# Hybrid decoder layer: the forgetting heads' bias is prepared on GpSimd without the query's factor, and ScalarE multiplies it in

## The chip, the cores and the metric

The kernel runs on one core of a Trainium2 chip. The metric is device time in microseconds (us) of one execution, the median of several. An execution's own time is a little longer than its span in the profile, which runs from the first to the last instruction of the program. The engines are named as the profile names them: PE is TensorE (PEld its weight loads), DVE is VectorE, ACT is ScalarE, POOL is GpSimd, SP is SyncE, which here only issues DMAs.

## The reference

One decoder layer over 512 tokens of width 2048, in float32: RMSNorm, one input projection, two groups of eight attention heads, an output projection with residual, a second RMSNorm and a SwiGLU feed-forward layer of width 5632 with residual. Eight heads (the NSA group) have compressed, selected and windowed branches. The other eight are the forgetting heads ("FoX"), and these are what the change is about:

```python
qf = _rms_norm(qf.reshape(B, T, Hf, Dh), fox_q_norm)
kf = _rms_norm(kf.reshape(B, T, Hf, Dh), fox_k_norm)
log_f = jax.nn.log_sigmoid(ff.astype(f32) + fox_forget_bias.astype(f32))
cum_f = jnp.transpose(jnp.cumsum(log_f, axis=1), (0, 2, 1))
...
s = jnp.einsum("bqhd,bkhd->bhqk", qf_b, kf).astype(f32) * scale
s = s + cq[..., None] - cum_f[:, :, None, :]
p = _masked_softmax(s, key_pos[None, :] <= tpos[:, None])
o_fox = jnp.einsum("bhqk,bkhd->bqhd", p.astype(dt), vf)
```

So each score gets a bias, the difference of two cumulative sums (of the query and of the key), and a causal mask, before the softmax.

## The kernel before

**Stages.** Up to about 370 us the kernel projects its input and runs the eight NSA heads beside it. From there to about 630 us it projects the forgetting heads' queries, keys and values, a pair of projections per head (`ps_kf`, `ps_qf`, `ps_vf`), and weaves the attention of the head before into them. Then comes the output projection (`po`), and from about 780 us the feed-forward layer (`q`, `pd`). Matrices are kept as a high and a low float32r part, so each product is three matmuls, and the large products are made by schemes with fewer multiplications whose operands are sums of blocks.

**One forgetting head.** `fox(h)` (L1005) first loads the row of cumulative sums, broadcast to 128 partitions, into `ckb` (one buffer for all heads; its DMA is issued from ACT's queue). `Branch.scores` (L737) then goes through the four blocks of 128 queries from the last, which has 512 keys, to the first, which has 128 (384 and 256 between). Per block: three matmuls write the scores `s_f` into a PSUM bank (two banks in turn, tag `s`); `nbs(i)` (L1010) makes the bias `nbf`; a DVE instruction reads both, scales by the query's factor, writes `p_f` and a row minimum `st_f`; ACT takes the exponential. So the matmuls of the third block need the bank of the first, and wait until DVE has read it. After the four blocks ACT multiplies `p_f` by the reciprocal sums (four instructions), PE transposes (`pT_f`) and multiplies by the values (`of`).

**The query's factor.** The queries are not normalised before the scores. `factors` (L590) makes, from the column sums `ss_qf`, the factor `qs` by which DVE multiplies at the end and its inverse `iqs`, by which the bias must be multiplied first. `qs_qf` is the tile of both. In `nbs` POOL adds the query's sum to `ckb` and multiplies by `iqs` in one TENSOR_SCALAR, then an AFFINE_SELECT writes a large number above the diagonal in the last 128 columns. There are two `nb` buffers.

**POOL's queue.** POOL also issues DMAs that add up blocks of weights in DRAM (`fsum`, `osum`, L279). Each is made to wait for a weight split on ACT, so that they are spread over the time; what stands behind one in POOL's queue waits with it.

**The order of instructions.** `Ordered` (L178) records what each of the five engines is given up to the end of the attention, and lays it out by five written lists of numbers (`ORDERS`, in the order PE, DVE, ACT, POOL, SP), at the top of the file. An engine works its list in order; the semaphores follow from the data. Behind that the order is the program's.

Of the kernel before, what the change touches and what calls it, by code (L numbers as in the profile page):

```python
# [10 lines left out]
F32 = mybir.dt.float32  # L11
FR = mybir.dt.float32r
AF = mybir.ActivationFunctionType
OP = mybir.AluOpType
# [4 lines left out]
P = 128  # L19
D = 2048  # L20
T = 512
# [3 lines left out]
NB = T // P  # L25
# [7 lines left out]
BIG = 1e30  # L33
# [192 lines left out]
def hybrid_layer(ctx: ExitStack, tc: tile.TileContext, xT, vec, ffb, wfg, wfirst, win, cmpw, wout, wos, wgu, wdn, out):  # L226
# [10 lines left out]
    def act(*args, **kw):  # L237
        return pin(sca.activation(*args, **kw))
# [13 lines left out]
    ap_ = att2.enter_context(tc.tile_pool(name="att", bufs=1))  # L252
# [2038 lines left out]
```

## Time and profile before

| | us |
|---|---|
| median of three executions (lowest to highest) | 2020.66 (2020.0 to 2022.35) |
| the profiled execution's own time | 2018.89 |
| its span | 2017.2 |
| PE busy | 1994.9 (99%) |
| DVE busy | 1794.1 (89%) |
| ACT busy | 1082.4 (54%) |
| POOL busy | 327.6 (16%) |

How to read it: matmuls overlap in the records and their ends are modelled, so PE's idle time in the profile is the time in which nothing at all was in flight. A wait is put down to the instruction whose semaphore came last. In a timeline the first column is the start in us from the span's start, the second the time that the merged group took, "x3" the number of instructions, and the bracket the engine's idle time before the group with what ended it.

### The profile page before, as it was taken

The page shows a single profiled execution, that of the slowest core. Times are in us where ns is not written, and L with a number is a line of the kernel's source. Part 1 is how long each engine was busy: PE and PEld are TensorE (multiplying, and loading weights), DVE is VectorE, ACT ScalarE, POOL GpSimd, SP SyncE. Part 2 cuts the span into 40 slices and gives each one's busy share as a digit, 9 for nine tenths or more (in the row PEclk, how much of TensorE's full clock was granted, in tenths as well). Part 3 has the DMA queues.
Part 4 walks back from the last instruction along what each step waited for, and adds up shares of the span by engine and source line. Part 5 has one row for each costly group of instructions (what it writes and reads, how often), then busy time and mean ns, then how long its engine had stood idle before and what let it go on. Part 6 is the DMA issues. An engine that isn't in the chain of part 4 may idle for free.

```text
span 2017.2 us, 36451 instructions
## 1 busy us (share of the span) xinstructions
PE 1994.9 (99%) x14341; PEld 1885.5 (93%) x14341; DVE 1794.1 (89%) x2725; ACT 1082.4 (54%) x1430; POOL 327.6 (16%) x481
## 2 busy tenths in 40 slices
PE   9999999999999998999999999999999999999999
PEld 8988989899998998999999999999999988888887
DVE  7788889898879777999999999999999998888897
ACT  6566566567676454444444443444444455666564
POOL 1132332423221011111111111111111000001000
PEclk9999999999999999999999999999999999999999
DMA  6676787967785674677767778778777798579974
GB/s 220 229 179 178 188 187 181 233 194 199 223 230 164 229 242 151 172 210 205 220 199 207 224 200 204 224 199 214 210 190 200 218 356 287 160 234 319 354 201 140
DMA packets 154062, 432.39 MB, mean 214 GB/s; under 512 B 18777, under 2 KB 26969, under 8 KB 153890
## 3 DMA queue, kind: packets, MB, share of 16 engines
q1 hardware_dynamic: 102176, 297.60, 44.7%
q0 software_dynamic: 44560, 106.19, 25.3%
q10 hardware_dynamic: 7154, 26.27, 3.4%
q8 instruction: 112, 1.84, 0.4%
q14 instruction: 60, 0.49, 0.1%
HBM read 393.54 MB, written 128.73 MB: 259 GB/s over the span
## 4 chain that ended last, share of the span: by engine, by line
PE 85%; issue 5%; DVE 4%; ACT 2%; POOL 2%; DMA 2%; SPq 0%; ACTq 0%; POOLq 0%; DVEq 0%
PE q L187 38%; PE pd L187 20%; PE po L187 8%; PE ps_qn L187 4%; PE ps_vf L187 2%; PE ps_vs L187 2%; PE ps_first L187 2%; PE on L187 2%; DVE bigm L187 1%; PE ps_kf L187 1%; POOL nbf L187 1%; PE ps_kw L187 1%; PE ps_ks L187 1%; PE s_s L187 1%; PE s_w L187 1%
## 5 line engine op out<-in xcount | busy, mean ns | idle before, releaser
L187 ACT ACTIVATE bigm<-r 128x1792 fp32r<-128x1792 f32 x174 | 299.2, 1720 | 416.7 <-PE q L187 273.5
L187 DVE TENSOR_TENSOR bigm<-r,bigm 128x1792 fp32r<-128x1792 f32 x174 | 351.2, 2019 | 2.6 <-ACT bigm L187 2.1
L187 DVE TENSOR_TENSOR r<-r 128x512 f32<-128x512 f32 x522 | 266.2, 511 | 20.5 <-DMA r<-wgu 8.4
L187 POOL DMA_DIRECT2D wsum<-wdn x176 | 120.3, 690 | 695.7 <-ACT bigm L187 602.2
L187 PE MATMUL q<-forma,bigm 128*128 128x256 f32 x1848 | 215.6, 276 | 4.5 <-ACT bigm L187 2.5
L187 PEld LDWEIGHTS q<-forma,bigm 128*128 128x128 f32 x1848 | 211.3, 193 | 5.3 <-ACT bigm L187 2.9
L187 PE MATMUL q<-formy,bigm 128*128 128x256 f32 x1848 | 214.1, 275 | 1.4 <-ACT bigm L187 1.1
L187 PE MATMUL q<-formx,bigm 128*128 128x256 f32 x1848 | 213.9, 275 | 0.0
L187 PE MATMUL q<-bigm 128*128 128x256 f32 x1848 | 213.8, 275 | 0.0
L187 PEld LDWEIGHTS q<-formy,bigm 128*128 128x128 f32 x1848 | 210.0, 192 | 1.8 <-ACT bigm L187 1.3
L187 PEld LDWEIGHTS q<-formx,bigm 128*128 128x128 f32 x1848 | 210.3, 192 | 0.0
L187 PEld LDWEIGHTS q<-bigm 128*128 128x128 f32 x1848 | 210.0, 192 | 0.2 <-DVE bigm L187 0.2
L187 PE MATMUL pd<-bigm 128*128 128x512 f32 x900 | 202.4, 379 | 0.0
L187 PEld LDWEIGHTS pd<-bigm 128*128 128x128 f32 x900 | 170.1, 189 | 24.2
L187 DVE TENSOR_TENSOR bigm<-wd,bigm 128x1024 fp32r<-128x1024 f32 (+1 forms) x62 | 107.7, 1738 | 21.5 <-ACT bigm L187 21.4
L187 ACT ACTIVATE bigm<-wd 128x1024 fp32r<-128x1024 f32 (+1 forms) x62 | 90.9, 1466 | 31.4 <-DMA wd<-wsum 26.3
L187 ACT ACTIVATE bigm<-rawm 128x768 fp32r<-128x768 f32 (+2 forms) x72 | 65.8, 923 | 64.6 <-PE pd L187 39.3
L187 PE MATMUL pd<-bigm,formx 128*128 128x512 f32 x444 | 99.3, 379 | 0.0
L187 PEld LDWEIGHTS pd<-bigm,formx 128*128 128x128 f32 x444 | 83.9, 189 | 11.9
L187 PE MATMUL po<-bigm,wp_o 128*128 128x512 f32 (+1 forms) x464 | 91.9, 348 | 0.7 <-DVE bigm L187 0.7
L187 DVE TENSOR_TENSOR bigm<-rawm,bigm 128x768 fp32r<-128x768 f32 (+2 forms) x72 | 75.5, 1058 | 16.8 <-ACT bigm L187 16.5
L187 PEld LDWEIGHTS po<-bigm,wp_o 128*128 128x128 f32 x464 | 76.8, 190 | 9.2 <-DVE bigm L187 1.1
(498 smaller groups left out, 3743.8 us busy)
## 6 DMA issues: line engine op xcount, KB each, us to landing
r<-wgu SPq DMA_DIRECT2D x174, 512.0 KB, 4.2
wsum<-wdn POOLq DMA_DIRECT2D x176, 256.0 KB, 5.0
rawm<-ad SPq DMA_DIRECT2D x44, 512.0 KB, 7.1
wd<-wdn SPq DMA_DIRECT2D x40, 512.0 KB, 5.9
wd<-wsum SPq DMA_DIRECT2D x40, 512.0 KB, 6.7
ad<-cb ACTq DMA_DIRECT2D x22, 896.0 KB, 5.9
fsump<-win POOLq DMA_DIRECT2D x72, 256.0 KB, 5.4
rawm<-ad SPq DMA_DIRECT2D x44, 384.0 KB, 3.4
```

The lines of the kernel that those rows point to most:

```text
L187: r = f(*args, **kw)
```

## The change

`fox(h)` now makes the biases of all four blocks when the head begins, in a dictionary `bias`, and without the query's factor: POOL adds (and multiplies by 1.0) and masks. `nbs(i)`, called where the scores are made, multiplies the finished bias in place on ACT by `iqs`, with an ACTIVATE Copy that has a scale per partition. The bias of 256 keys gets a buffer of its own (`nb1`), and that of 128 keys takes the last 128 columns of the buffer of the 384 keys, so that a head's four biases fit at one time. Four of the five lists of the order are written anew (SP's is the same).

```diff
--- before.py
+++ after.py
-0+1 6+4 2+2 91 11+1 99 5 13 15 14 17 20 18 16 19 22 21 23 26 29 24 32 25 28 27 35 38 41 30 44 31 34 33 47 50 37
+0+1 6+3 3+1 91 11+1 99 10 2 5 13 15 14 17 20 18 16 19 22 21 23 26 29 24 32 25 28 27 35 38 41 30 44 31 34 33 47
...
+        bias = {}
+        for i in reversed(range(NB)):
+            n = P * (i + 1)
+            if i == 1:
+                nbt = ap_.tile([P, 2 * P], F32, tag="nb1", name=f"nbf{h}{i}", bufs=1)
+            elif i > 1:
+                nbt = both = ap_.tile([P, T], F32, tag="nb", name=f"nbf{h}{i}", bufs=2)
+            nb = bias[i] = nbt[:, :n] if i else both[:, 3 * P:]
+            pool.tensor_scalar(nb, ck[:, :n], ncq[:, i, h:h + 1], 1.0, op0=OP.add, op1=OP.mult)
+            pool.affine_select(nb[:, n - P:], nb[:, n - P:], pattern=[[-1, P]], compare_op=OP.is_ge,
+                                    fill=BIG, base=0, channel_multiplier=1)
+
         def nbs(i):
-            n = P * (i + 1)
-            nb = ap_.tile([P, T], F32, tag="nb", name=f"nbf{h}{i}", bufs=2)
-            pool.tensor_scalar(nb[:, :n], ck[:, :n], ncq[:, i, h:h + 1], q[2][:, i:i + 1] if len(q) == 3 else 1.0, op0=OP.add, op1=OP.mult)
-            pool.affine_select(nb[:, n - P:n], nb[:, n - P:n], pattern=[[-1, P]], compare_op=OP.is_ge,
-                                    fill=BIG, base=0, channel_multiplier=1)
-            return nb[:, :n]
+            if len(q) == 3:
+                act(bias[i], bias[i], AF.Copy, scale=q[2][:, i:i + 1])
+            return bias[i]
```

The lists of numbers show nothing by themselves; here are the places that matter, as the built programs have them. The number behind a tile's name is a buffer's and differs between the programs.

POOL around head 2's bias. Before, behind the DMAs that belong to the split of the next weights:

```order
L187 DMA osum_127<-wos 128x512
L187 DMA osum_128<-wos 128x512 x2
L187 DMA osum_129<-wos 128x512 x2
L187 DMA osum_126<-wos 128x512 x2
L187 TENSOR_SCALAR nbf_5516<-ckb_5499,ncq,qs_qf_5468 128x512
L187 TENSOR_SCALAR nbf_5539<-ckb_5499,ncq,qs_qf_5468 128x384
L187 AFFINE_SELECT nbf_5516<-nbf_5516 128x128
L187 AFFINE_SELECT nbf_5539<-nbf_5539 128x128
```

And in the change:

```order
L188 DMA osum_127<-wos 128x512
L188 TENSOR_SCALAR nbf_5519<-ckb_5505,ncq 128x512
L188 AFFINE_SELECT nbf_5519<-nbf_5519 128x128
L188 DMA osum_127<-wos 128x512
L188 TENSOR_SCALAR nbf_5529<-ckb_5505,ncq 128x256
L188 AFFINE_SELECT nbf_5529<-nbf_5529 128x128
L188 DMA osum_128<-wos 128x512
L188 TENSOR_SCALAR nbf_5524<-ckb_5505,ncq 128x384
L188 TENSOR_SCALAR nbf_5524<-ckb_5505,ncq 128x128
L188 AFFINE_SELECT nbf_5524<-nbf_5524 128x128 x2
L188 DMA osum_128<-wos 128x512
```

The bias no longer reads `qs_qf`, and it has moved ahead of seven `osum` DMAs: its first instruction now stands after the 147th DMA of POOL's queue, where it stood after the 154th.

ACT at the same place. Before, the first rows after head 2's factors (the `wp` rows are splits of projection weights):

```order
L187 ACTIVATE qs_qf_5468<-qs_qf_5468 128x4 x3
L187 ACTIVATE wp_kf_6_5567<-ws_pair_6_5363 128x1024
L187 ACTIVATE wp_kf_0_5619<-ws_pair_0_5409 128x1024
L187 ACTIVATE p_f_5513,st_f_5514<-p_f_5513,st_f_5514 128x512
L187 ACTIVATE p_f_5513,st_f_5514<-p_f_5513,st_f_5514 128x384
L187 DMA ckb_5861<-cumd 128x512
L187 ACTIVATE p_f_5513,st_f_5514<-p_f_5513,st_f_5514 128x256
```

And in the change:

```order
L188 ACTIVATE qs_qf_5474<-qs_qf_5474 128x4 x3
L188 ACTIVATE kf_5431<-t_kf_4935 128x512
L188 DMA od_209<-o_5483 128x512
L188 ACTIVATE wp_kf_6_5580<-ws_pair_6_5369 128x1024
L188 ACTIVATE nbf_5519<-nbf_5519,qs_qf_5474 128x512
L188 ACTIVATE nbf_5524<-nbf_5524,qs_qf_5474 128x384
L188 ACTIVATE nbf_5524<-nbf_5524,qs_qf_5474 128x128
L188 ACTIVATE nbf_5529<-nbf_5529,qs_qf_5474 128x256
L188 ACTIVATE wp_kf_0_5628<-ws_pair_0_5415 128x1024
L188 ACTIVATE p_f_5538,st_f_5539<-p_f_5538,st_f_5539 128x512
L188 ACTIVATE p_f_5538,st_f_5539<-p_f_5538,st_f_5539 128x384
L188 ACTIVATE p_f_5538,st_f_5539<-p_f_5538,st_f_5539 128x256
```

The four multiplications stand between the factors and the next weight split, and the DMA of the next head's `ckb` is gone from among the exponentials.

ACT in the middle of head 0. Before:

```order
L187 ACTIVATE p_f_4469,st_f_4470<-p_f_4469,st_f_4470 128x384
L187 ACTIVATE f_7_4538<-d_7_4463 128x256
L187 DMA ckb_4947<-cumd 128x512
L187 ACTIVATE wp_vf_1_4678<-ws_vf_1_4676 128x1024
L187 ACTIVATE p_f_4469,st_f_4470<-p_f_4469,st_f_4470 128x256
```

And in the change:

```order
L188 ACTIVATE p_f_4488,st_f_4489<-p_f_4488,st_f_4489 128x384
L188 ACTIVATE f_7_4549<-d_7_4463 128x256
L188 ACTIVATE wp_vf_1_4681<-ws_vf_1_4679 128x1024
L188 ACTIVATE p_f_4488,st_f_4489<-p_f_4488,st_f_4489 128x256
L188 ACTIVATE kf_4546<-t_kf_4419 128x512
```

The DMA of head 1's `ckb` stood here in ACT's queue, ahead of a weight split; in the change it stands before head 0's factors, behind the first `pt_w` of the last NSA head.

159 rows, old and new, of the table ORDERS are left out of this document.

## The prediction

> **What bounds the kernel now.** First the page's first part, then the windows, then the waits of PE by themselves.
>
> ```profile
> PE 1994.9 (99%) x14341; PEld 1885.5 (93%) x14341; DVE 1794.1 (89%) x2725; ACT 1082.4 (54%) x1430; POOL 327.6 (16%) x481
> ```
>
> ```profile
> 300.00:350.00 50.00, 50.00 (x371) 47.35 (x370) 48.12 (x126) 32.14 (x79) 14.45 (x24) 1.00 0.70 180
> ...
> sum 230.00, PE 220.17 PEld 210.24 DVE 191.69 ACT 163.68 POOL 75.09; mean PE 27.52 PEld 26.28 DVE 23.96 ACT 20.46 POOL 9.39
> ```
>
> PE bounds the program: it stands idle for 2017.2 - 1994.9 = 22.3 us in all. The windows (columns: stretch, its length, then PE, PEld, DVE, ACT, POOL busy) show where. Just ahead of the forgetting heads PE is full; the eight windows that hold these heads (366 to 436 without 396 to 408, 454 to 626; the sum row is theirs) have 230.0 - 220.2 = 9.8 us of its idle time. Who ends the idle time says the list of waits for PE (total, times, longest):
>
> ```profile
> PE q L187 <- ACT bigm L187: 3.6, 2, 2.5
> PE s_f L187 <- DVE st_f L187: 3.4, 5, 0.9
> PE q L187 <- DVE bigm L187: 2.2, 2, 2.0
> PE ps_vf L187 <- DVE f L187: 2.0, 1, 2.0
> PE pT_f L187 <- ACT p_f L187: 1.4, 2, 0.7
> PE ps_vf L187 <- ACT wp_vf L187: 1.3, 1, 1.3
> ```
>
> The two `q` rows belong to the feed-forward layer. The other four, 3.4 + 2.0 + 1.4 + 1.3 = 8.1 us in nine waits, are all in the heads' stretch. What is saved there reaches the end: the chain's last two pieces are PE alone,
>
> ```profile
> 904.15 710.08 PE q L187 x6356
> 1614.23 398.88 PE pd L187 x1848
> ```
>
> so everything behind moves forward with it. A matmul of 256 columns takes 710.08 / 6356 = 0.112 us when nothing holds it.
>
> **The five waits of `s_f`: the bias is late.** Head 2 as an example, timelines of PE, DVE, POOL and ACT, one after the other:
>
> ```profile
> 460.16 0.50 PE L187 MATMUL ps_kf<-f,wp_kf 128*128 128x256 f32 x3
> 461.52 0.62 PE L187 MATMUL s_f<-kf,qq 128*128 128x256 f32 x3 [0.86 <-DVE st_f L187]
> 461.98 0.27 PE L187 MATMUL ps_kf<-f,wp_kf 128*128 128x256 f32 x1
> ```
>
> ```profile
> 457.51 0.16 DVE L187 SCALAR_TENSOR_TENSOR qs_qf<-qs_qf 128x4 f32<-128x4 f32 x1
> ...
> 457.92 1.21 DVE L187 TENSOR_TENSOR wq_kf<-ws_pair,wp_kf 128x1024 fp32r<-128x1024 f32 x1
> 460.71 0.75 DVE L187 CUSTOM_DVE_ANT_0 p_f<-s_f,nbf,qs_qf 128x512 f32<-128x512 f32 x1 [1.57 <-POOL nbf L187]
> ```
>
> ```profile
> 457.94 2.48 POOL L187 TENSOR_SCALAR nbf<-ckb,ncq,qs_qf 128x512 f32<-128x512 f32 x2
> 460.39 0.54 POOL L187 TENSOR_SCALAR_AFFINE_SELECT nbf<-nbf 128x128 f32<-128x128 f32 x2
> ```
>
> ```profile
> 458.94 1.06 ACT L187 ACTIVATE wp_kf<-ws_pair 128x1024 fp32r<-128x1024 f32 x1 [1.89 <-PE ps_kf L187]
> 461.50 0.72 ACT L187 ACTIVATE p_f<-p_f,st_f 128x512 f32<-128x512 f32 x1 [1.51 <-DVE st_f L187]
> ...
> 468.06 1.91 ACT L187 ACTIVATE p_f<-p_f,st_f 128x128 f32<-128x128 f32 x4
> ```
>
> DVE finishes the factor at 457.67. POOL starts on it at once, but two TENSOR_SCALARs stand before the first AFFINE_SELECT, so the bias of 512 keys comes at about 460.7. DVE has stood idle for 1.57 us, reads the bank until 461.46, and PE, which had nothing left at 460.66, goes on at 461.52.
>
> The change leaves one ACT instruction between factor and bias. The trace has no ACT multiplication of `nbf`, but it has the same instruction on another tile: four Copies with a scale per partition on `p_f`, of 128, 512, 256 and 384 columns, 1.91 us together (last row). One of 512 columns costs between 0.48 (a mean quarter) and 0.72 us (the exponential of that size); I take 0.72. ACT is idle at 457.67, so the bias is there at about 458.4; DVE's split ends at 459.13, so `p_f` runs at 459.13 instead of 460.71 and the bank is free at 459.9, 0.8 us before PE needs it. The new limit is DVE's split, and it takes DVE's whole 1.57 us of waiting away. In heads 3 and 6 the new list puts these score matmuls eight rows of 256 columns (0.9 us) earlier; there a tenth may stay. Saved: 3.4 - 0.2 = 3.2 us.
>
> **The two waits in head 0: ACT behind POOL behind a DMA.** Timelines of POOL, ACT and PE:
>
> ```profile
> 388.87 0.83 POOL L187 DMA_DIRECT2D osum<-osum  x1 [3.55 <-DMA osum<-wos]
> 389.46 0.73 POOL L187 TENSOR_SCALAR nbf<-ckb,ncq,qs_qf 128x128 f32<-128x128 f32 x1
> 390.26 0.29 POOL L187 TENSOR_SCALAR_AFFINE_SELECT nbf<-nbf 128x128 f32<-128x128 f32 x1
> ```
>
> ```profile
> 390.22 0.33 ACTq L187 DMA_DIRECT2D ckb<-cumd  x1
> 390.65 1.06 ACT L187 ACTIVATE wp_vf<-ws_vf 128x1024 fp32r<-128x1024 f32 x1 [4.13 <-POOL nbf L187]
> ```
>
> ```profile
> 391.76 1.60 PE L187 MATMUL ps_vf<-wp_vf,bigm 128*128 128x256 f32 x12 [1.26 <-ACT wp_vf L187]
> 395.36 2.05 PE L187 MATMUL ps_vf<-wp_vf,bigm 128*128 128x256 f32 x16 [2.00 <-DVE f L187]
> ```
>
> POOL waits 3.55 us for a weight sum to land before it makes head 0's last bias. Head 1's `ckb` may overwrite the one buffer only then, its DMA is issued from ACT's queue, so ACT stands for 4.13 us, and PE runs out of split weights, then of a PSUM bank whose readers on ACT and DVE were delayed too. In the change that bias is made in the NSA stage and the DMA has left this place. ACT gets four multiplications, up to 1.91 us, ahead of it, against 4.13 that go: 2.2 us of margin, more than PE's longest wait of 2.00. Saved: 1.3 + 2.0 = 3.3.
>
> **The two waits of `pT_f`, and refilling.** These transposes wait for ACT's last multiplications of `p_f`. The exponentials move forward by up to DVE's 1.57 us, but PE arrives about 0.9 earlier as well, and ACT has 1.91 us more to do. I take half, 0.7 us; the bounds are 0 and 1.4. After a wait PE also restarts slowly: the three `s_f` of head 2 took 461.98 - 461.52 = 0.46 us against 3 x 0.112 = 0.34. Eight waits fewer at 0.12 are 1.0 us.
>
> **What it adds.** ACT: 8 heads x 1.91 = 15.3 us. ACT's idle time in the eight windows is 230.0 - 163.7 = 66.3, and at head 2 it stands idle from 457.05 to 458.94: of the 1.91 us from 457.67 on, 1.27 are covered there, and 1.51 more are idle at 461.50. Cover gone, they delay the next `wp` split and with it PE, at worst by 1.91 per head. I charge half of one such pack, 1.0 us; bounds 0 and 15.3. POOL: as many instructions as before, and earlier. Head 2's biases now stand behind the 147th to the 149th DMA of its queue, the first of which is this one, and read a `ckb` that is issued a head earlier (its row: count, size, us to landing):
>
> ```profile
> 417.31 0.57 POOL L187 DMA_DIRECT2D osum<-wos  x1 [5.55 <-ACT wp_kf L187]
> ```
>
> ```profile
> ckb<-cumd ACTq DMA_DIRECT2D x8, 256.0 KB, 4.7
> ```
>
> That is forty us ahead of 457.94, when POOL begins them now, and a landing takes 4.7. What queues behind these waits on POOL are weight sums, which no row shows as late for PE.
>
> **A lock that moves along.** DVE and POOL hold each other up in this trace:
>
> ```profile
> 375.93 1.42 POOL L187 TENSOR_SCALAR nbf<-ckb,ncq,qs_qf 128x512 f32<-128x512 f32 x2
> 377.31 2.66 POOL L187 TENSOR_SCALAR_AFFINE_SELECT nbf<-nbf 128x128 f32<-128x128 f32 x2
> ```
>
> ```profile
> 376.45 1.45 DVE L187 TENSOR_TENSOR sb_kf<-t_kf 64x512 f32<-64x512 f32 x1
> 378.00 0.68 DVE L187 TENSOR_TENSOR sq_kf<-sq_kf,sb_kf 64x512 f32<-64x512 f32 x1
> ```
>
> A DVE instruction beside POOL's took 1.45 instead of 0.68, 0.77 us more, and POOL's selects 1.33 each instead of 0.27 at head 2. The Trainium skill, "SBUF — State Buffer", section "SBUF: two separate sides", has a rule for it: the port pair that DVE and GpSimd share is held by one instruction as a whole, also against DVE instructions with two SBUF inputs, while ScalarE has its own ports. The trace agrees in kind. By it POOL's bias work is no cheaper for DVE early than late, only elsewhere: the sum would be the 1.0 us of the first rival below, where the rows of PE's waits give 7.2.
>
> **The sum.** 3.2 + 3.3 + 0.7 + 1.0 - 1.0 = 7.2 us. The profiled execution goes from 2018.89 to 2011.7. It lies 1.8 under the median of the three runs shown (2020.66), so the median goes to 2013.5.
>
> **Rivals.** (1) The lock moves: in each of eight heads one DVE instruction on PE's path is held for 0.77 us, 6.2 us in all, and 1.0 us of the gain is left: 2019.7. For it: both rows above. Against it: most of DVE's work there does not end a wait of PE (8.1 us of such waits in all). (2) The new lists open waits elsewhere. Four of five are new from the start of the program, and 300 to 350 us has nothing to win and can only lose; four waits of 0.9, the size of the present ones, cost 3.6 and leave 2017.1. (3) Slower: ACT becomes what PE waits for. The four multiplications stand ahead of the next weight split; where ACT has no idle time after the factor, the split comes 1.91 us later and PE waits for it. It decides from the point where this happens in five of the eight heads (9.6 us against 8.2 gained); in all eight it is 15.3 - 8.2 = 7.1 more, 2027.8. Against it: ACT's 66 us of idle time, and the 1.27 + 1.51 at head 2. (4) It doesn't do what it says: POOL's bias is still late, behind an `osum` wait, and ACT waits in its stead; then only head 0's 3.3 us are won, 2017.4. Against it: the forty us of lead.
>
> **Chances.** The forecast 0.68, rivals (1) 0.09, (2) 0.12, (3) 0.07, (4) 0.04. The likeliest case alone reaches from 2010.1 (no charge on ACT, all of `pT_f`, and the other 9.8 - 8.1 = 1.7 us of idle time) to 2016.4 (no gain at `pT_f` and in refilling, and 2.2 us of charge instead of 1.0). The range takes in the first, second and fourth rival: 2010 to 2019.8. A difference under 0.2% (4 us) can't be told from none, so faster means under 2016.6: 0.69, the forecast and a little of the rivals; the same 0.24; slower 0.07.
>
> **What would show it.** In the profile after, `s_f <- DVE st_f` and `ps_vf <- ACT wp_vf` are gone from PE's waits, DVE's `p_f <- POOL nbf` (here 1.57 in head 2) is gone too, and ACT has 32 more instructions and some 15 us more. If DVE then waits for `ACT nbf`, or ACT for `POOL nbf`, the fourth rival holds; if PE waits for `wp` rows, the third. PE idle in the eight heads' windows should fall from 9.8 to 3 or 4 us. The forecast is wrong if PE's idle time falls and the time doesn't, or if new waits of PE stand before 366 us.

## The result, and the profile after

Five executions of the changed kernel took 2006.23, 2007.47, 2011.66, 2011.93 and 2012.08 us, median 2011.66, against 2020.0 for the kernel before (five executions). The ratio is 0.9949, 95% interval [0.9933, 0.9965], which is 10.3 us less, where the forecast had 7.2 (2013.5). Ten later executions, in two other comparisons, gave 0.9943 both times ([0.993, 0.9955] and [0.993, 0.9957]), 11.5 us less. The profiled execution took 2011.93; the forecast for it was 2011.7. That agreement is an accident, as the following rows show.

The page's first part, and the list of waits for PE, of the changed kernel:

```profile
PE 1993.3 (99%) x14341; PEld 1886.0 (94%) x14341; DVE 1794.6 (89%) x2725; ACT 1095.7 (55%) x1462; POOL 317.3 (16%) x481
```

```profile
PE q L188 <- ACT bigm L188: 5.3, 2, 2.8
PE q L188 <- DVE tmp_r L188: 3.7, 1, 3.7
PE ps_warm L188 <- DVE onesf L188: 1.1, 1, 1.1
PE ps_kf L188 <- DVE bigm L188: 0.8, 1, 0.8
...
PE ps_vf L188 <- ACT wp_vf L188: 0.2, 1, 0.2
```

All nine waits that the forecast wanted gone are gone (`s_f`, `pT_f <- ACT p_f`, both large `ps_vf`). A new one of 3.7 us, `q <- DVE tmp_r`, stands at the entry of the feed-forward layer, a place that the forecast did not look at. In the forecast's own eight windows PE's idle time is now 230.00 - 228.59 = 1.4 us, where 3 to 4 had been forecast. Small new waits of PE stand before 366 us (0.4 at `zr_vc`, 0.3 and 0.2 at `ps_first`), which the forecast had named as a sign of being wrong; the two repetitions of the change below have none of them, so they do not belong to it.

To compare the heads' stretch without the shift of time, it is cut at the same matmuls in both programs: the first `s_f` of the heads 0 to 6, the first `po`, the last `po` (head 7's first `s_f` falls into the row of head 6). Of before, the rows of head 0, of head 2, of the output projection, and the sum over all eight rows (stretch, length, busy time of PE, PEld, DVE, ACT, POOL):

```profile
379.13:418.35 39.22, 35.97 (x279) 34.46 (x278) 32.97 (x69) 22.65 (x49) 15.48 (x22) 1.00 0.72 188
...
456.92:483.61 26.69, 25.15 (x209) 24.09 (x207) 20.95 (x43) 19.76 (x39) 9.30 (x13) 1.00 0.76 202
...
610.69:778.61 167.92, 166.60 (x1032) 152.65 (x1031) 135.10 (x197) 93.22 (x123) 19.80 (x36) 1.00 0.61 195
sum 399.48, PE 388.74 PEld 367.71 DVE 329.20 ACT 259.01 POOL 88.68; mean PE 48.59 PEld 45.96 DVE 41.15 ACT 32.38 POOL 11.09
```

And of the changed kernel:

```profile
379.80:415.31 35.51, 35.51 (x280) 34.38 (x279) 32.08 (x69) 23.88 (x51) 11.31 (x18) 1.00 0.81 202
...
453.95:478.52 24.57, 24.57 (x208) 24.01 (x207) 22.18 (x46) 22.09 (x43) 8.48 (x13) 1.00 0.86 231
...
600.84:767.12 166.28, 166.28 (x1033) 152.77 (x1031) 133.71 (x193) 93.69 (x124) 15.82 (x29) 1.00 0.60 196
sum 387.32, PE 385.90 PEld 367.17 DVE 327.93 ACT 271.44 POOL 76.01; mean PE 48.24 PEld 45.90 DVE 40.99 ACT 33.93 POOL 9.50
```

The stretch became 399.48 - 387.32 = 12.2 us shorter, not 7.2. PE's idle time fell from 399.48 - 388.74 = 10.7 to 1.4, by 9.3 us, and the same matmuls took 388.74 - 385.90 = 2.8 us less of busy time. The rest of the program gave some of it back. The feed-forward layer from its first `q` to its last, before and after:

```profile
781.47:1613.95 832.48, 829.04 (x7395) 828.01 (x7396) 801.98 (x1077) 349.93 (x255) 120.31 (x176) 1.00 0.75 205
```

```profile
770.05:1606.98 836.93, 830.04 (x7395) 829.28 (x7396) 802.45 (x1077) 348.44 (x255) 120.00 (x176) 1.00 0.75 204
```

4.45 us are lost there, and the stretch began 379.80 - 379.13 = 0.7 later. 12.2 - 4.45 - 0.7 = 7.0, the difference of the spans (2017.2 and 2010.2).

Of the fifteen executions of the changed kernel, eight lie between 2006.2 and 2008.4 and seven between 2009.9 and 2012.1. The profile above is of the upper group; the two later profiles of the change are of the lower, and neither has the `tmp_r` wait.

### The profile page after: what moved, and what is told of

Its sections match the earlier page's. It is cut to its first block, busy times and chain, and to the rows that moved or that the text cites. A ratio compares the mean times of both kernels' runs of the same rounds, so it can differ in the third digit from the quotient of the medians.

```text
span 2010.2 us, 36451 instructions
## 1 busy us (share of the span) xinstructions
PE 1993.3 (99%) x14341; PEld 1886.0 (94%) x14341; DVE 1794.6 (89%) x2725; ACT 1095.7 (55%) x1462; POOL 317.3 (16%) x481
## 4 chain that ended last, share of the span: by engine, by line
PE 96%; issue 1%; DVE 1%; DMA 1%; ACT 0%; POOL 0%; SPq 0%; POOLq 0%; DVEq 0%; ACTq 0%
PE q L188 40%; PE pd L188 20%; PE po L188 8%; PE ps_kf L188 6%; PE ps_qn L188 4%; PE ps_vf L188 4%; PE ps_vs L188 2%; PE ps_first L188 2%; PE on L188 2%; PE ps_kw L188 1%; PE ps_qf L188 1%; PE ps_ks L188 1%; PE s_s L188 1%; PE of L188 1%; PE s_w L188 1%
```

## The experiments

Two theories. A: the late bias is the whole matter, and the forecast's 7.2 us is right. B: more is won in the heads' stretch than its rows held, part of it by the new lists, and part is lost again where the feed-forward layer begins. The third rival of the prediction, ACT as what PE waits for, is tried by itself.

### The change again

> The changed kernel once more, unaltered, beside the next three. Theory A (the forecast's sum is right, 7.2 us): its median lies some 7 us under that of the kernel before. Theory B (more is won in the heads' stretch than the forecast's rows hold, and part is lost again where the feed-forward layer begins): PE's `q` waits near 807 us, 3.7 us in the first profile of the change, are there in the slower executions and missing in the faster ones, so the times fall into two groups some 4 us apart, and the median is 8 to 10 under before.

Measured: median 2007.75 (2006.4 to 2010.92), ratio 0.9943 [0.993, 0.9955]. The profiled execution took 2007.29, span 2005.6, and its list of waits for PE has no `tmp_r` row; the first two are:

```profile
PE q L188 <- ACT bigm L188: 5.2, 2, 2.7
PE q L188 <- DVE bigm L188: 1.8, 1, 1.8
```

The stretch from the first `s_f` to the last `po` is as short as in the first profile (387.90), the feed-forward layer takes 832.53. So the gain in the heads repeats. The times fall apart again (2009.9 and 2010.92 against 2006.4 to 2007.75), as they would if the loss behind the heads were there in some executions only; just one execution of this run has a profile. The median is lower than either theory had it. The 0.7 us at the start are missing too; they do not belong to the change.

### The mechanism with the old lists

The changed code; PE's and DVE's lists are those of before, ACT's and POOL's too but for what the change moves. ACT around a head's factor, in short:

```diff
 ACTIVATE qs_qf2<-qs_qf2 x3
+ACTIVATE nbf2<-nbf2,qs_qf2 x4
+DMA ckb3<-cumd
 ACTIVATE wp_kf4<-ws_pair2
 ...
 ACTIVATE p_f2<-p_f2,st_f2
-DMA ckb3<-cumd
```

> The mechanism alone: biases on POOL at the head's start, four multiplications on ACT right after the factor, the next head's cumulative sums loaded behind them; every other instruction stands where it stood before. Theory A (the late bias is the whole matter): all of the gain, 7 to 10 us under the kernel before, and no wait of `s_f` and none of `ps_vf` behind ACT in head 0. Theory B (the re-made lists bring a share of their own): 4 to 6 us under before, with the small waits of PE in the heads' stretch that the lists removed still there. Rival (ACT becomes what PE waits for, which the new lists avoid): no faster than before.

Measured: median 2010.06, ratio 0.9953 [0.994, 0.9965], 9.5 us under before. The same eight stretches, their sum, and the waits of PE that are not in the changed kernel:

```profile
sum 390.37, PE 386.48 PEld 366.95 DVE 329.70 ACT 271.88 POOL 79.33; mean PE 48.31 PEld 45.87 DVE 41.21 ACT 33.98 POOL 9.92
```

```profile
PE of L186 <- ACT vf L186: 1.3, 1, 1.3
...
PE ps_kf L186 <- DVE t_kf L186: 0.8, 1, 0.8
PE ss_kf L186 <- DVE fr_kf L186: 0.4, 2, 0.2
```

Theory A had 7 to 10, B 4 to 6: A's size holds, and so does B's sign that small waits stay. 9.1 us of the 12.2 in the profiles come from the mechanism alone: 6.85 of idle time and 2.26 of busy time. Of the small waits that the forecast left at nothing, `t_kf` is still there and `ss_kf` at half, and a new one of 1.3 us stands at `vf`, behind the first `po`. Counted from the first `po`, PE reaches that point 1.2 us earlier than before and ACT has `vf` ready 0.4 us later (7.8 us behind it, before 7.5), so the larger part of it is PE coming sooner. With the new lists `vf` and `ss_kf` are gone; `t_kf` has only given way to a wait of the same length in the same head (`ps_kf <- DVE bigm`, 0.8).

### The new lists with the old bias

The kernel before with the change's order for PE, DVE and ACT. POOL's whole list is that of before, with the bias in its old places, and the load of `ckb` keeps its place in ACT's queue. So three of the four new lists are tried here.

> The four new lists with the old bias: POOL adds and multiplies by the factor at the old places, ACT multiplies nothing, and the load of the next head's cumulative sums stands where it stood in ACT's queue. Theory A: within 1 us of the kernel before, since all its waits are still there. Theory B: 2 to 5 us under before. Rival (the lists fit the new bias only): 1 to 4 us over before.

Measured: median 2021.88, ratio 1.0007 [0.9998, 1.0017], 1.4 us over before (0.4 under to 3.4 over). Theory A had within 1 us of before, the rival 1 to 4 over: the interval takes in both, and theory B (2 to 5 under) is out. Head 0 and the sum of the eight stretches:

```profile
379.04:419.33 40.29, 37.58 (x279) 36.09 (x278) 32.51 (x69) 21.99 (x47) 16.13 (x23) 0.96 0.71 184
...
sum 399.81, PE 390.77 PEld 369.20 DVE 327.83 ACT 258.41 POOL 86.94; mean PE 48.85 PEld 46.15 DVE 40.98 ACT 32.30 POOL 10.87
```

By themselves the lists win little in the heads. The sum is that of before (399.81 against 399.48), but head 0 ran at a granted clock of 0.96 in this execution, and PE was busy there for 1.6 us more than before; the other seven rows are 0.7 us shorter, and PE's idle time in all eight is 9.0 instead of 10.7. The feed-forward layer takes 836.39: `q <- DVE tmp_r` is there, 3.3 us. Together with the early bias the lists bring more (390.37 with the old lists against 387.32 and 387.90 with the new, 2.5 to 3.1 us), and the loss behind the heads comes with them: the mechanism with the old lists does not have that wait.

### One DMA

```diff
 ACTIVATE f4<-d4
-DMA ckb1<-cumd
 ACTIVATE wp_vf2<-ws_vf2
 ...
 ACTIVATE f5<-d4
 ACTIVATE fr_qf1<-sq_qf1
+DMA ckb1<-cumd
 ACTIVATE p_f0<-p_f0,st_f0
```

> The kernel before with one entry of ACT's list moved: the load of head 1's cumulative sums stands ten entries later, behind head 0's last exponential, so that ACT no longer waits 4.13 us for POOL there. Theory A: 3.3 us under before, PE's waits `ps_vf <- ACT wp_vf` (1.3) and `ps_vf <- DVE f` (2.0) gone, everything behind earlier by that. If the five waits of `s_f` in later heads are unchanged, 3.4 us of them remain in the list. Rival (ACT is late there for another reason): under 1 us.

Measured: median 2016.16, ratio 0.9981 [0.9972, 0.999], 3.8 us under before (2.0 to 5.7). Head 0, cut as above:

```profile
379.78:415.53 35.75, 35.71 (x280) 34.39 (x279) 32.80 (x69) 22.77 (x49) 15.61 (x22) 1.00 0.78 207
```

39.22 became 35.75, 3.5 us less; PE's idle time there fell from 3.25 to 0.04. The `s_f` row of the waits is the old one, 3.4 in five. Moving one load ten entries down ACT's list is a third of what the change won.

### No lead for POOL

```diff
             pool.affine_select(nb[:, n - P:n], nb[:, n - P:n], pattern=[[-1, P]], compare_op=OP.is_ge,
                                     fill=BIG, base=0, channel_multiplier=1)
+            if len(q) == 3:
+                act(nb[:, :n], nb[:, :n], AF.Copy, scale=1.0)
             return nb[:, :n]
```

> The kernel before with ACT's 32 multiplications, but without POOL's lead: POOL adds, multiplies by the query's factor and masks where it did, and ACT multiplies the finished bias by 1.0 behind it. Every list is otherwise that of before. Theory A (the lead of POOL is what gains): no gain in the heads 2 to 7, the waits of `s_f` longer than the 3.4 us of before by 0.5 to 0.7 each, and the whole 2 to 10 us slower than before. Rival (the load that moves in ACT's queue, or the new order, is what gains): no slower than before.

Measured: median 2025.59, ratio 1.0027 [1.0017, 1.0037], 5.5 us over before. PE's waits for `s_f`, and DVE and ACT at head 2's first bias:

```profile
PE s_f L188 <- DVE st_f L188: 7.5, 6, 1.5
```

```profile
462.20 0.75 DVE L188 CUSTOM_DVE_ANT_0 p_f<-s_f,nbf,qs_qf 128x512 f32<-128x512 f32 x1 [2.23 <-ACT nbf L188]
```

```profile
461.54 1.04 ACT L188 ACTIVATE nbf<-nbf 128x512 f32<-128x512 f32 x2 [0.71 <-POOL nbf L188]
```

DVE's 1.57 us became 2.23, and the waits of `s_f` grew by 4.1 us, somewhat more than the 0.5 to 0.7 each that was expected. With ACT's multiplication but without the lead the change is a loss. So the lead is what removes the waits of `s_f`; this is what the fourth rival would have looked like. In the change itself no wait of DVE for `nbf` is left.

### ACT's multiplications twice and four times

```diff
                 act(bias[i], bias[i], AF.Copy, scale=q[2][:, i:i + 1])
+                for _ in range(1):
+                    act(bias[i], bias[i], AF.Copy, scale=1.0)
```

(`range(3)` for four times.)

> The changed kernel with each of ACT's 32 multiplications of the bias followed by a second one, by 1.0: 1.9 us more of ACT per head, 15 in all. The forecast charged 1.0 us for the first set. Theory A (ACT's idle time hides it nearly whole): 0 to 2 us over the change, and it says that the charge should have been near nothing. Rival (ACT is close to being what PE waits for: the third rival of the prediction): about 1.9 us for each head in which no idle time is left behind the factor, 8 to 15 us over the change, and waits of PE for weight splits of ACT in the heads' stretch.

> The same with three more of each, 46 us more of ACT in all, 5.7 per head. Theory A: ACT's idle time of 46 us in the eight windows is then used up on paper, and the weight splits come late in most heads: 10 to 30 us over the change, more than three times the cost of one more. Rival (linear from the start): three times what one more costs.

Measured: twice 2017.88, ratio 0.9992 [0.9984, 1.0001]; four times 2055.77, ratio 1.0178 [1.0164, 1.0192]. Against the change that is some 10 us for the second set, 1.2 per head, and some 47 for three. With two sets the rival's size held (8 to 15), not its place: PE waits at the transposes most, hardly for weight splits. With four, theory A's shape held (more than three times the cost of one set) and its place, though the cost lies over its 10 to 30: now PE waits for weight splits, 6.2 and 4.7 us. So a second set costs two thirds of its length, and three sets cost all of theirs. The kernel with two sets, then that with four:

```profile
PE pT_f L189 <- ACT p_f L189: 3.8, 9, 0.7
```

```profile
PE ps_kf L189 <- ACT wp_kf L189: 6.2, 4, 3.0
...
PE ps_vf L189 <- ACT wp_vf L189: 4.7, 4, 2.1
```

Why the first set was free and the second is not can be read at head 2. ACT's last multiplications of `p_f` and PE's transposes of them, in the change (the second profile):

```profile
463.50 1.91 ACT L188 ACTIVATE p_f<-p_f,st_f 128x128 f32<-128x128 f32 x4
```

```profile
465.23 0.67 PE L188 MATMUL pT_f<-ident,p_f 128*128 128x128 f32 x4
```

And with two sets:

```profile
466.72 1.91 ACT L189 ACTIVATE p_f<-p_f,st_f 128x128 f32<-128x128 f32 x4
```

```profile
467.16 0.33 PE L189 MATMUL pT_f<-ident,p_f 128*128 128x128 f32 x1
468.17 0.33 PE L189 MATMUL pT_f<-ident,p_f 128*128 128x128 f32 x1 [0.68 <-ACT p_f L189]
```

In the change ACT is done with the four at 465.41 and PE begins to read them at 465.23. There is no room left there; with the second set PE stands 0.68 us at the second of them. In the two longest heads (1 and 4, 38.6 and 42.6 us) the second set cost under 0.2 us.

### The entry of the feed-forward layer

There DVE's list in the change has the first sum of the ninth weight load ahead of the split of the eighth and of the first `tmp_r`; before it stood behind both. PE waits for the `tmp_r`. DVE and PE in the first profile of the change:

```profile
803.92 0.69 DVE L188 TENSOR_TENSOR ca<-q,e_g 128x512 f32<-128x512 f32 x1
808.04 0.69 DVE L188 TENSOR_TENSOR r<-r 128x512 f32<-128x512 f32 x1 [3.43 <-DMA r<-wgu]
808.65 2.02 DVE L188 TENSOR_TENSOR bigm<-r,bigm 128x1792 fp32r<-128x1792 f32 x1
810.58 0.42 DVE L188 SCALAR_TENSOR_TENSOR tmp_r<-q,tmp_r 128x256 f32<-128x256 f32 x1
```

```profile
811.05 3.59 PE L188 MATMUL q<-formy,bigm 128*128 128x256 f32 x16 [3.71 <-DVE tmp_r L188]
```

The load was issued at 800.12; the view of its tile gives its way to the landing:

```profile
DMA to landing us min/median/max: 7.9/7.9/7.9
```

In the second profile the load took 5.5, and nothing waited. The edit, in DVE's list:

```diff
 TENSOR_TENSOR ca<-q0,e_g0
-TENSOR_TENSOR r8<-r8
 TENSOR_TENSOR bigm<-r7,bigm
 SCALAR_TENSOR_TENSOR tmp_r2<-q1,tmp_r2
+TENSOR_TENSOR r8<-r8
 TENSOR_TENSOR r8<-r8 x2
```

> The changed kernel with one instruction of DVE's list put back two places, where it stood before the change: the first sum of the ninth weight load of the feed-forward layer, now behind the split of the eighth and behind the first `tmp_r`. The change's DVE list has it ahead of both, so that where this load lands late (at 37.97 us after the first `q`, against 35.11 in the other profile of the change), DVE waits, and PE behind it 3.7 us. Theory B (this place in the list turns a late load into a wait of PE): the wait `q <- DVE tmp_r` is gone in every execution, the group of executions near 2011 to 2012 is gone, the highest lies under 2010, and the median 1 to 3 us under the change's. Rival (the load is late because a weight sum's DMA starts beside it, and whoever uses it waits): the wait shows up again behind another DVE instruction, and the times are those of the change.

Measured: median 2008.23 (2006.96 to 2010.07), ratio 0.9943 [0.9929, 0.9956]. The highest is over the 2010 that was expected, the load landed early in the profiled execution (4.8 us), and the changed kernel had not been run beside it: nothing was told apart. So both were run together, with one more kernel: in its POOL list the weight sum that can start just ahead of that load changes places with the next.

```diff
 DMA wsum0<-wdn
-DMA wsum1[0]<-wdn
 DMA wsum1[1]<-wdn
+DMA wsum1[0]<-wdn
 DMA wsum2[0]<-wdn
```

> The changed kernel once more, for its next two beside it. Its ten executions so far lie between 2006.2 and 2012.1, five of them over 2009.8. Theory B (DVE's list at the entry of the feed-forward layer turns a late load into a wait of PE of 2 to 4 us): about half of the executions again over 2009.8, median near 2009. Rival (the spread is that of any kernel here): a spread like that of the kernel before, 5 us, without two groups.

> The kernel with the first sum of the ninth weight load put back behind the split of the eighth, once more, since its first five executions (2007.0 to 2010.1) beside no others of the change left it open. Theory B: a median 1 to 2 us under the change's of the same call, at most one execution in five over 2009.8. Rival: the same median as the change within 0.5 us.

> The same, and in POOL's list the weight sum that can start just ahead of that load (at 29.8 us after the first `q` in the slower profile, at 30.9 in the faster) changes places with the next one, so that it starts some 5 us later. If it is this DMA beside it that makes the load land at 37 to 38 us instead of 34.6 to 35.1, the load lands early in every execution: median like the last kernel's or up to 1 us lower, and a narrower spread. Rival (the crowding only moves to the next load): no gain over the last, or up to 3 us slower.

Measured: the change 2008.44 (2006.68 to 2011.41), ratio 0.9943 [0.993, 0.9957]; with the sum put back 2007.39 (2005.35 to 2008.16), 0.9932 [0.992, 0.9944]; with the DMAs exchanged too 2007.26 (2006.19 to 2007.8), 0.9933 [0.992, 0.9945]. This time the load was late in the profiled execution of the second, issued at 798.66 and 7.1 us under way. Its DVE and PE:

```profile
803.27 2.03 DVE L188 TENSOR_TENSOR bigm<-r,bigm 128x1792 fp32r<-128x1792 f32 x1
805.21 0.42 DVE L188 SCALAR_TENSOR_TENSOR tmp_r<-q,tmp_r 128x256 f32<-128x256 f32 x1
805.80 1.61 DVE L188 TENSOR_TENSOR r<-r 128x512 f32<-128x512 f32 x3 [0.18 <-DMA r<-wgu]
```

```profile
803.22 4.85 PE L188 MATMUL q<-formy,bigm 128*128 128x256 f32 x42
```

DVE waits 0.18 us for it in place of 3.43, and PE not at all. Two of the five executions of the change lie over 2009.8 and none of the second kernel, whose median is 1.05 lower, as theory B has it. Of the six profiles with the list as the change has it, four have the `tmp_r` wait (the change 3.7, the lists alone 3.3, two and four sets of multiplications 1.9 and 3.3); of the seven with the old place none has it, though the load was late in four of them too (before 7.0 us, one DMA 8.1, no lead 7.1, this one 7.1). Of fifteen executions of the change seven took over 2009.8 us, of fifteen with the sum put back (five of them with the DMAs exchanged too) one did; the means are 2009.1 and 2007.5. The place in the list as the cause of the wait is shown; the gain of 1 to 1.6 us is likely, but not shown: the ratios' intervals overlap, and the granted clock is a rival for differences of this size. The second kernel's profiled execution, the fastest of all (2005.35), ran through this entry at 1.00 (five windows of ten us from 766.5 us on), the change's beside it at 0.83, 0.88 and 0.95 in the first three such windows from 767.0 on. In the third kernel the load took 4.6 us, and its five times lie closer together (1.6 us apart, the second's 2.8); the median did not change, so the rival to this step (no gain over the last) stands.

## Why the prediction was right or wrong

The mechanism held, and the size did not. The medians of the two repetitions, 2007.75 and 2008.44, lie under 2010, the lower end of the forecast's range. The step that failed is the sum for the heads' stretch: 7.2 us were forecast and 12.2 measured. Three of its terms were mis-sized: restarting (1.0 forecast, 2.8 measured), the charge on ACT (1.0 forecast, none measured in the change), and two kinds of short waits that the sum put at nothing (1.5 us at `ss_kf` and `po`, all gone). The 0.9 us that it held back at `s_f` and `pT_f` went too. A fourth term is missing: the entry of the feed-forward layer, where up to 4.5 us are lost again.

The eight stretches hold all steps of the sum, so they can be set against it (us of time won):

| step of the forecast | forecast | mechanism, old lists | change |
|---|---|---|---|
| idle time of PE, the waits less the charge on ACT (3.2 + 3.3 + 0.7 - 1.0) | 6.2 | 6.85 | 9.3 |
| restarting after waits, in PE's busy time | 1.0 | 2.3 | 2.8 |
| sum | 7.2 | 9.1 | 12.2 |
| entry of the feed-forward layer | 0 | -0.1 | 0 to -4.5 |

**What bounds it: right; "what is saved there reaches the end": not in every execution.** PE's idle time in the heads went, and in the lower group of executions what was saved there reached the end. The forecast took this from the chain's last two pieces, but they begin at 904.15 us. Ahead of them, at the entry of the feed-forward layer, the chain of before goes through a weight load:

```profile
786.79 5.85 DMA r<-wgu
```

There an order that waits for a later load of this kind can take the gain back.

**The waits of `s_f`: right.** The row is gone. DVE's new limit is its split, as the step said: at head 2 (second profile of the change) it goes from the split straight to `p_f`, without a wait.

```profile
454.41 1.22 DVE L188 TENSOR_TENSOR wq_kf<-ws_pair,wp_kf 128x1024 fp32r<-128x1024 f32 x1
455.54 0.75 DVE L188 CUSTOM_DVE_ANT_0 p_f<-s_f,nbf,qs_qf 128x512 f32<-128x512 f32 x1
```

**Head 0: right.** 3.3 was forecast for its two waits; the one DMA alone gave 3.5 in the profile and 3.8 (2.0 to 5.7) in time.

**"After a wait PE also restarts slowly": right in kind, too small.** 0.12 us for each of eight waits was read from the three matmuls that follow one wait. The busy time of PE over the whole stretch fell by 2.8 us, and it fell where waits went: by 0.46, 0.58, 0.43, 0.58 and 0.47 in the heads 0, 2, 3, 5 and 6 and by 0.32 in the output projection, but by less than 0.1 up or down in the heads 1 and 4, where none went. Twelve waits are gone in those six rows (nine of the forecast, two of `ss_kf`, one of `po`), so one costs 0.24 us beside its idle time. The granted clock reads 1.00 in all these rows, so it is not the clock. A part can be seen in the rows of the prediction: the single matmul at 461.98 is busy for 0.27 us, where one in a row adds 0.112, so an estimated 0.16 us of it stand alone each time that PE runs empty. The ends of matmuls are modelled, and what the rest is made of stays open.

**The charge on ACT, 1.0: in the change it is not there.** The price of the multiplications was right, to 0.01 us per head (1.92 for 1.91):

```profile
454.19 1.92 ACT L188 ACTIVATE nbf<-nbf,qs_qf 128x512 f32<-128x512 f32 x4 [0.55 <-DVE qs_qf L188]
```

On the whole page ACT's busy time rose by 13.3 us, somewhat less than the 15 forecast. With the old lists 0.4 us of lateness of ACT shows up, in the wait at `vf`; the new lists avoid it. But the step's reason was wrong: 66 us of idle time in the windows do not say that ACT can take more. It could take this one set, and about a third of a second.

**`pT_f`, half of 1.4: all of it went.** At head 2 ACT's last multiplication is done just as PE needs it (465.41 against 465.23), so there is some luck in it.

**"The new lists open waits elsewhere": half right.** From 300 to 350 us, where this rival looked, they opened none. In the heads the change took away waits that the sum had left at nothing: `ss_kf` (0.8) and `po` (0.7). The third of this kind, `t_kf` (0.7), was replaced by `ps_kf <- DVE bigm` (0.8), and head 1 is as long as before. Both repetitions also have a new `pT_f <- DVE pt_f` of 0.5 to 0.6 us in the heads, as has the kernel with the lists alone (0.4). Of before:

```profile
PE ss_kf L187 <- DVE fr_kf L187: 0.8, 2, 0.6
PE ps_kf L187 <- DVE t_kf L187: 0.7, 1, 0.7
PE po L187 <- DVE bigm L187: 0.7, 1, 0.7
```

They opened the largest where nobody looked, behind the heads: 3.7 us at `q`. By the times it is there in some seven of fifteen executions, but only three of the fifteen have a profile. In the first profile the errors cancelled, which is luck; in the lower group of executions the change wins 13 us rather than 7.

**The lock between DVE and POOL: not seen.** POOL's work moved, and DVE's busy time in the eight stretches is 329.20 before, 329.70 with the mechanism and the old lists, and 327.93 after; over the whole program it is 1794.1 before and 1794.6 after.

**ACT as what PE waits for: wrong for this change, one set of multiplications away from right.** Its price, 1.91 per head in the worst case, was 1.2 on average for the second set.

## What to carry to other kernels

An engine's idle time in a stretch says little about what it can still take; look at how long before its use the last result is ready at the point where the busy engine reads it (here 0 us for ACT's `p_f` after the change). The load issued from ACT's queue made all of ACT wait for the load's buffer (4.13 us), so such a load belongs behind the work that frees the buffer: one entry moved was worth 3.5 us. And where an order is written by hand, an instruction that needs a load should not stand ahead of one that the bounding engine waits for: such an order costs something only in those executions in which the load is late.

## What the runs showed of the hardware

A 512 KB load that was issued within 0.3 us of an accumulating weight sum on POOL's queue took 6.5 to 8.1 us to land in eight profiles (among them before, 7.0, and the change, 7.9), and 4.6 to 5.5 where the weight sum started 0.8 us or more behind it (both repetitions of the change, the mechanism alone, the first run with the sum put back, the DMAs exchanged). Which it is differs between executions of the same program. That the weight sum is the cause is not shown: the kernel that moves it has one profile.

PE's pace after a pause of the same length differs too. The first 28 `q` of the feed-forward layer, in the mechanism with the old lists and in the second profile of the change:

```profile
772.23 5.02 PE L186 MATMUL q<-forma,bigm 128*128 128x256 f32 x28 [2.49 <-ACT bigm L186]
```

```profile
769.82 3.39 PE L188 MATMUL q<-forma,bigm 128*128 128x256 f32 x28 [2.55 <-ACT bigm L188]
```

The granted clock over six us there was 0.72 in the one and 1.00 in the other (the third value from the end):

```profile
772.00:778.00 6.00, 5.42 (x31) 5.24 (x32) 4.54 (x6) 3.00 (x4) 1.09 (x2) 0.72 0.35 129
```

```profile
769.00:775.00 6.00, 3.40 (x29) 3.21 (x29) 4.13 (x6) 3.28 (x4) 1.07 (x2) 1.00 0.44 160
```

The Trainium skill, "TensorE: Matmul & The Clock Gate", section "What's actually happening", says that the array falls to half its clock after an idle window of some 3.4 us, and that this window runs freely, so that the point differs from run to run. The difference between executions agrees with that; the pause ahead of the slow matmuls here, 2.49 us, is shorter than the window, so an idle window of the page's length is not what this trace shows.
